# Both ends of a tree-attention kernel: codes fetched once, first V copies regrouped, one pair in other PSUM, three late stores on hardware queues

## The chip, the cores and the metric

The kernel runs on one core of one Trainium2 chip. The metric is the device time of one execution in microseconds; lower is better. Before the change the median of five runs is 138.11 us (137.77 to 138.54).

## What is computed

Attention over a binary tree: query i sees only itself and its ancestors. The shapes are 8 batches x 12 heads, 512 positions, 64 elements, all float32.

```python
mask = np.zeros((seq, seq))
for i in range(seq):
    mask[i, i] = 1
    parent = i
    while parent > 0:
        parent = (parent - 1) // 2
        mask[i, parent] = 1
scores = np.einsum('bhqd,bhkd->bhqk', Q, K) * scale
scores = scores + (1 - mask) * (-1e9)
weights = np.exp(scores - np.max(scores, axis=-1, keepdims=True))
weights = weights / (np.sum(weights, axis=-1, keepdims=True) + 1e-10)
return np.einsum('bhqk,bhkd->bhqd', weights, V)
```

## The kernel before

The 96 heads form 48 pairs (two heads, the unit of compute), 24 quads (four heads, the unit of a store) and 12 octets (eight heads, the unit of a V load and of the tile `vt`). Position n of a head sits on partition n // 4, slot n % 4, so one partition of one head is 1 KB in HBM.

For each pair i:
- `transpose(i)` (L280) makes 16 TensorE transposes of K and Q with the permutation tile `ptile` into the PSUM tile `kqp`; `evac(i)` (L293) copies it to SBUF on DVE.
- `scores1` and `scores2` (L309, L331): TensorE adds a product of mask codes (tiles `codes`, two copies on partitions 0 and 64 on, one for each head of a pair) and a product of keys and queries in PSUM, and ACT takes the exponential. No score matrix of 512x512 is made: a query sees at most ten keys, and the keys are sorted so that two groups of 128 are enough for each query tile.
- `values(i)` (L354): 20 products with 65 columns, the 65th a column of ones that gives the sum; they go to the PSUM tile `ob`, of which the pool has one.
- `norm(i)` (L380): DVE takes the reciprocal of the sums and multiplies into the output tile `of`.

V is not used as it was loaded. For each octet, copies bring rows of `vst` to where the products want them in `vt`: `spread_top` on POOL (L223), `spread_leaves` on DVE (L237), `spread_l7` on DVE or ACT (L250). Octet 0 is done in two halves by `spread_first` (L443); `spread_vector` (L451) says what DVE copies at which pair.

The order is written out by hand and no scheduler moves it. The main loop (L477) has at step i: scores of pair i, an ACT copy for some i, values and norm of pair i - 1, transposes of pair i + 2, DVE copies for some i, and further steps of POOL's program. The POOL program (L409) issues all K, Q and V loads but the first, which convert float32 to bfloat16 on the way, with 8 software DMAs at most under way, and all stores but the last; quad q is stored 8 quads behind its loads. After the last load come quads 14 to 17, the copies of octet 11, and quads 18 to 22. The last quad goes by SP (heads 0 and 1, then head 2) and ACT (head 3).

At the start SP and ACT load the first pair of K and Q, the permutations and both copies of the codes, while TensorE runs 12 products of zeros (`busy`, L474).

Of the kernel before, what the change touches and what calls it, by code (L numbers as in the profile page):

```python
# [41 lines left out]
KTOP, KLOW = 8, 40  # L42
# [61 lines left out]
def _permutations():  # L104

    eye = np.eye(128, dtype=np.float32)
    return np.concatenate([eye[:, r:r + 32] for r in PERMS], axis=1)


def _run(order):  # L110
    at = [n for n in range(len(PERMS) - 3) if PERMS[n:n + 4] == tuple(order)][0]
    return slice(32 * at, 32 * at + 128)
# [3 lines left out]
def kernel(  # L116
# [7 lines left out]
    nc = tc.nc  # L124
    B, H, S, D = Q.shape
    P = nc.NUM_PARTITIONS
    assert S == 512 and D == 64 and P == 128 and (B * H) % 4 == 0
    scale = float(1.0 / np.sqrt(D))
    NQ = B * H // 4
    NP = 2 * NQ  # L130

    fp32 = mybir.dt.float32
# [10 lines left out]
    perm_dram, top_dram, low_dram = (  # L143
        nc.inline_tensor(a.astype(ml_dtypes.bfloat16), name=name)
        for a, name in (
            (_permutations(), "permutations"), (top_np, "codes_top"), (low_np, "codes_low"),
        )
    )
# [11 lines left out]
    psT = ctx.enter_context(tc.tile_pool(name="psT", bufs=1, space=bass.MemoryType.PSUM))  # L160
    psO = ctx.enter_context(tc.tile_pool(name="psO", bufs=1, space=bass.MemoryType.PSUM))


    ptile = consts.tile([P, 32 * len(PERMS)], bf16)
    first = [consts.tile([P, 2, 4, D], fp32, name=f"first_{n}") for n in "kq"]
    codes = [
        consts.tile([P, a.shape[1]], bf16, name=f"codes_{n}")
        for n, a in enumerate((top_np, low_np))
    ]
    for tile_codes in codes:  # L170
        nc.vector.memset(tile_codes[:, :], 0.0)
    for eng, st, src in ((nc.sync, first[0], Kr), (nc.scalar, first[1], Qr)):
        eng.dma_start(out=st[:, :, :, :].rearrange("p h t d -> p h (t d)"), in_=src[:, 0:2, :])
    nc.sync.dma_start(out=ptile[:, :], in_=perm_dram.ap())
    for eng, half in ((nc.sync, 0), (nc.scalar, 64)):
        eng.dma_start(out=codes[0][half:half + KTOP, :], in_=top_dram.ap())
        eng.dma_start(out=codes[1][half:half + KLOW, :], in_=low_dram.ap())
    qperm = ptile[:, _run((0, 32, 64, 96))]
    perms = [ptile[:, _run(_slot_layout(t)[0])] for t in range(4)]
    k1code, q1code = codes[0][:, 0:128], codes[0][:, 128:640]  # L180
# [22 lines left out]
    qTs, kTs, kqps, obs, ets, ofs = {}, {}, {}, {}, {}, {}  # L203
# [10 lines left out]
    def load_k(o, h0=0, n=8):  # L214
        load(ksts, "kst", loads, Kr, o, h0, n)

    def load_q(o, h0=0, n=8):
        load(qsts, "qst", loads, Qr, o, h0, n)

    def load_v(o, h0=0, n=8):  # L220
        load(vsts, "vst", vloads, Vr, o, h0, n)
# [8 lines left out]
    def tile_pair(o, p, h0, h1, first):  # L230

        c, step = VCOL[first], VCOL[first + 2] - VCOL[first]
        return vts[o % NV][p:p + 64, h0:h1, c:c + 2 * step].rearrange(
            "p h (t d) -> p h t d", t=2
        )[:, :, :, 0:D]

    def spread_leaves(o, upper, h0=0, h1=8):  # L237

        nc.vector.tensor_copy(  # L239
            out=tile_pair(o, 64 if upper else 0, h0, h1, upper),  # L240
            in_=vsts[o][64:128, h0:h1, upper:3 + upper:2, :],
        )

    def swapped(src, step):

        return bass.AP(
            src.tensor, src.offset, [list(src.ap[0]), list(src.ap[1]), [step, 2], [1, D]]
        )

    def spread_l7(copy, o, quad, h0=0, h1=8):  # L250

        slot = 2 * (quad % 2)
        lower = quad < 2
        copy(  # L254
            out=tile_pair(o, 0, h0, h1, 1)[32 * quad:32 * quad + 32] if lower
            else tile_pair(o, 64, h0, h1, 0)[32 * quad - 64:32 * quad - 32],
            in_=swapped(vsts[o][32:64, h0:h1, slot + (not lower), :], D if lower else -D),
        )

    def busy(n):  # L260

        ob = psO.tile([P, 2, 512], fp32, name="ob")
        for _ in range(n):
            nc.tensor.matmul(  # L264
                out=ob[:, 0, :], lhsT=zeros[:, 0:128], rhs=zeros[:, :], start=True, stop=True
            )
# [86 lines left out]

    def values(i):  # L354

        obs[i] = ob = psO.tile([P, 2, 512], fp32, name="ob")
        e1, e2, vt = ets[i], e2s[i % NE], vts[(i // 4) % NV]

        def product(e, a, t, col, lo=0, hi=128, **flags):

            start_o = 65 * t + (t >= 2)
            col -= t < 2
            nc.tensor.matmul(  # L363
                out=ob[lo:hi, a, start_o:start_o + 65],
                lhsT=e[:, a, QPOS[t], lo:hi],
                rhs=vt[:, 2 * (i % 4) + a, col:col + 65],
                **flags,
            )

        for a in range(2):  # L370
            for t in range(4):
                product(e1, a, t, VTOP, start=t == 0, stop=False)
            for t in (2, 3):
                product(e2, a, t, VCOL[t], start=False, stop=False)
        for a in range(2):
            for t in (0, 1):
                product(e2, a, t, VCOL[SELF[t]], 0, 64, start=False, stop=t == 1)
                product(e2, a, t, VCOL[t], 64, 128, start=False, stop=t == 1)
# [20 lines left out]
    def store(eng, q, h0=0, n=4):  # L399
        eng.dma_start(  # L400
            out=Or[:, 4 * q + h0:4 * q + h0 + n, :],
            in_=ofs[q][:, h0:h0 + n, :, :].rearrange("p h t d -> p h (t d)"),
        )
# [3 lines left out]
    NO = NQ // 2  # L407

    def pool_program():  # L409

        load_k(0, 2, 2)
        load_q(0, 2, 2)
        load_v(0, 0, 4)
        load_k(0, 4, 4)
        load_q(0, 4, 4)
        load_v(0, 4, 4)
        load_k(1, 0, 4)
        load_q(1, 0, 4)
        spread_top(nc.gpsimd, 0, 0, 4)
        load_v(1)  # L420
        load_k(1, 4, 4)
        load_q(1, 4, 4)
        spread_top(nc.gpsimd, 0, 4, 8)
        yield
        yield
        for o in range(2, NO):
            load_k(o, 0, 4)
            load_q(o, 0, 4)
            load_v(o)
            load_k(o, 4, 4)  # L430
            spread_top(nc.gpsimd, o - 1)
            load_q(o, 4, 4)
            yield
            for q in (2 * o - BEHIND, 2 * o + 1 - BEHIND):
                if q >= 0:
                    store(nc.gpsimd, q)
        for q in range(NQ - BEHIND, NQ - 1):
            yield
            store(nc.gpsimd, q)
            if q == NQ - BEHIND + 1:  # L440
                spread_top(nc.gpsimd, NO - 1)

    def spread_first(quad, parts):  # L443

        for part in parts:
            if part < 4:
                spread_l7(nc.vector.tensor_copy, 0, part, 4 * quad, 4 * quad + 4)
            else:
                spread_leaves(0, part - 4, 4 * quad, 4 * quad + 4)

    def spread_vector(i):  # L451

        if i == 1 or i == 2:
            spread_first(1, range(3) if i == 1 else range(3, 6))
        o, step = divmod(i + 2, 4)
        if 1 <= o < NO:
            if step == 0:
                spread_leaves(o, 0)
            elif step == 1:
                spread_leaves(o, 1)  # L460
                for quad in (2, 3):
                    spread_l7(nc.vector.tensor_copy, o, quad)

    def pool_until(done, wanted):
        while done < wanted:
            next(program, None)
            done += 1
        return done
# [2 lines left out]
    steps = pool_until(0, 1)  # L471
    nc.vector.tensor_copy(out=ksts[0][:, 0:2, :, :], in_=first[0][:, :, :, :])
    nc.scalar.copy(out=qsts[0][:, 0:2, :, :], in_=first[1][:, :, :, :])
    busy(12)  # L474
    transpose(0)
    evac(0)
    for i in range(NP + 1):  # L477
        if i < NP:
            scores1(i)
            scores2(i)  # L480

            o, quad = divmod(i + 1, 4)
            if 1 <= o < NO and quad < 2:
                spread_l7(nc.scalar.copy, o, quad)
        if i == 1:
            transpose(2)
            evac(2)
            spread_first(0, range(4, 6))
        if i >= 1:
            values(i - 1)  # L490
            norm(i - 1)
        for n in (1 if i == 0 else i + 2,):
            if n < NP:
                transpose(n)
                evac(n)
        if i == 0:
            spread_first(0, range(4))
        spread_vector(i)
        if steps < NO:
            steps = pool_until(steps, min((i + 11) // 4, NO))  # L500
        else:
            steps = pool_until(steps, min(steps + 2, NO + (i - 2) // 2 - (NQ - 1 - BEHIND)))
        if i == NP - 1:
            store(nc.sync, NQ - 1, 0, 2)
    store(nc.sync, NQ - 1, 2, 1)
    store(nc.scalar, NQ - 1, 3, 1)

# [29 lines left out]
```

## Time and profile before

| what | value |
|---|---|
| median of five runs | 138.11 us |
| the profiled execution: its time, its span | 137.95 us, 135.9 us |
| busy: PE, DVE, ACT, POOL | 112.7, 103.7, 105.6, 95.3 us |
| read from HBM, written to it | 37.92 MB, 12.58 MB |
| DMA packets: software queue, two hardware queues | 30.68 MB; 0.77 and 0.44 MB |
| PE's waits for V copies on DVE | 3.3 us, 4 times |
| last Q load: issued; PE goes on with it | 110.99 us, 121.30 us |
| last multiply ends | 131.15 us |

The span runs from the first to the last instruction; about 2.05 us of the execution lie outside it. DMA shares can be over 1 because packets of one engine overlap. A row of the timeline has the start, the duration, the engine, the line, what it writes and reads, and in brackets what ended the idle time before it. A row of issues in the DMA view has the size and the time from issue to landing.

### The profile page before, as it was taken

How to read it: one execution, taken by the hardware profiler on the slowest of the kernel's cores; microseconds unless marked ns; L12 is line 12 of the kernel's file. 1: busy time of each engine (PE TensorE's matmuls, PEld its weight loads, DVE VectorE, ACT ScalarE, POOL GpSimd, SP SyncE). 2: the span in 40 equal slices, each digit the busy share in tenths (PEclk: the TensorE clock that was granted, in tenths of full speed). 3: DMA queues.
4: the chain of work that ended last, by engine and by line, in shares of the span. 5: the costliest groups of instructions: out<-in, count | busy, mean ns of one | idle time of the engine just before them, and what ended most of it. 6: DMA issues, size and time to landing. Idle time of an engine off the chain costs nothing.

```text
span 135.9 us, 5536 instructions
## 1 busy us (share of the span) xinstructions
PE 112.7 (83%) x2412; PEld 80.4 (59%) x2412; DVE 103.7 (76%) x220; ACT 105.6 (78%) x121; POOL 95.3 (70%) x140
## 2 busy tenths in 40 slices
PE   4985939999899898998998997997998697969620
PEld 1344716767576676775686674765766576747310
DVE  6139798879879879599698798898797878797520
ACT  3236554989989989989899899798899878898700
POOL 6969969397797975972985796596597597294200
PEclk9999995999999999999999999999999999999965
DMA  3999999999999999999999999999999999999981
GB/s 125 202 188 195 196 196 197 198 196 198 196 198 236 321 200 205 347 198 200 345 202 198 320 234 196 303 253 198 283 272 198 258 300 198 246 378 380 370 311 49
DMA packets 42043, 32.23 MB, mean 237 GB/s; under 512 B 1476, under 2 KB 39076, under 8 KB 42020
## 3 DMA queue, kind: packets, MB, share of 16 engines
q0 software_dynamic: 40640, 30.68, 124.6%
q1 hardware_dynamic: 898, 0.77, 1.7%
q10 hardware_dynamic: 482, 0.44, 1.0%
q8 instruction: 18, 0.29, 0.8%
q14 instruction: 5, 0.04, 0.1%
HBM read 37.92 MB, written 12.58 MB: 372 GB/s over the span
## 4 chain that ended last, share of the span: by engine, by line
PE 37%; ACT 22%; DMA 17%; DVE 14%; issue 4%; POOL 2%; ACTq 0%
PE ob L363 12%; DMA vst<-in_V_dram 9%; ACT e L324 9%; DMA qst<-in_Q_dram 8%; ACT e L348 7%; PE kqp L276 7%; ACT vt L254 5%; PE s L313 4%; PE ob L264 4%; PE s L335 4%; DVE of L392 4%; DVE vt L254 4%; PE s L342 3%; PE s L318 3%; DVE kq L302 3%
## 5 line engine op out<-in xcount | busy, mean ns | idle before, releaser
L324 ACT ACTIVATE e<-s 128x1024 bf16<-128x1024 f32 x48 | 49.0, 1021 | 17.1 <-PE s L318 16.3
L363 PE MATMUL ob<-vt,e 128*128 128x65 bf16 (+1 forms) x960 | 39.3, 198 | 10.2 <-DVE of L392 6.4
L363 PEld LDWEIGHTS <-e 128*128 128x128 bf16 (+1 forms) x960 | 31.1, 103 | 17.1 <-PE s L342 6.6
L348 ACT ACTIVATE e<-s 128x768 bf16<-128x768 f32 x48 | 38.4, 801 | 0.0
L225 POOL COPY vt<-vst 32x512 bf16<-32x512 bf16 (+1 forms) x52 | 31.0, 597 | 10.4 <-DMA vst<-in_V_dram 8.4
L302 DVE COPY kq<-kqp 128x1024 bf16<-128x1024 bf16 x48 | 32.7, 682 | 5.4 <-PE kqp L276 5.4
L392 DVE TENSOR_TENSOR of<-ob,rec 128x512 f32<-128x512 f32 x48 | 33.2, 692 | 1.7
L209 POOL DMA_DIRECT2D kst<-in_K_dram x24 | 18.3, 763 | 12.3 <-DMA vst<-in_V_dram 10.4
L254 ACT COPY vt<-vst 32x1024 bf16<-32x1024 bf16 x22 | 22.8, 1036 | 2.6 <-DVE vt L239 2.3
L389 DVE RECIPROCAL rec<-ob 128x8 f32<-128x8 f32 x48 | 9.9, 207 | 16.5 <-PE ob L363 15.6
L276 PE MATMUL kqp<-ptile,kst 128*64 128x128 bf16 x384 | 19.6, 222 | 1.5 <-issue 1.5
L209 POOL DMA_DIRECT2D qst<-in_Q_dram x24 | 18.2, 758 | 2.8 <-PE s L342 1.2
L400 POOL DMA_DIRECT2D out_dram<-of x23 | 17.4, 762 | 3.6 <-DVE of L392 3.2
L276 PE MATMUL kqp<-ptile,qst 128*64 128x128 bf16 x384 | 19.1, 221 | 1.0 <-DMA qst<-in_Q_dram 1.0
L318 PE MATMUL s<-kq 64*128 64x512 bf16 x96 | 19.0, 381 | 1.0 <-DVE kq L302 0.7
L313 PE MATMUL s<-codes 64*128 64x512 bf16 x96 | 19.0, 389 | 1.0 <-ACT e L324 0.2
L342 PEld LDWEIGHTS <-kq 64*128 64x128 bf16 x384 | 16.1, 95 | 5.0 <-issue 0.4
L342 PE MATMUL s<-kq 64*128 64x96 bf16 (+3 forms) x384 | 17.9, 211 | 0.0
L254 DVE COPY vt<-vst 32x1024 bf16<-32x1024 bf16 (+1 forms) x30 | 16.6, 553 | 0.7
L335 PE MATMUL s<-codes 64*128 64x384 bf16 x96 | 16.2, 328 | 1.0
L335 PEld LDWEIGHTS <-codes 64*128 64x128 bf16 x96 | 7.6, 94 | 12.6 <-issue 6.0
L276 PEld LDWEIGHTS <-qst 128*64 128x64 bf16 x384 | 13.7, 111 | 1.2 <-DMA qst<-in_Q_dram 1.2
(20 smaller groups left out, 59.1 us busy)
## 6 DMA issues: line engine op xcount, KB each, us to landing
out_dram<-of POOLq DMA_DIRECT2D x23, 512.0 KB, 10.5
kst<-in_K_dram POOLq DMA_DIRECT2D x23, 256.0 KB, 11.4
qst<-in_Q_dram POOLq DMA_DIRECT2D x23, 256.0 KB, 9.6
vst<-in_V_dram POOLq DMA_DIRECT2D x11, 512.0 KB, 12.6
vst<-in_V_dram POOLq DMA_DIRECT2D x2, 256.0 KB, 6.3
first_q<-in_Q_dram ACTq DMA_DIRECT2D x1, 256.0 KB, 3.6
first_k<-in_K_dram SPq DMA_DIRECT2D x1, 256.0 KB, 3.3
out_dram<-of SPq DMA_DIRECT2D x1, 256.0 KB, 4.8
```

The source lines that it names most:

```text
L209: nc.gpsimd.dma_start(out=kept[o][:, h0:h0 + n, :, :].rearrange("p h t d -> p h (t d)"), in_=src[:, 8 * o + h0:8 * o + h0 + n, :],)
L225: eng.tensor_copy(out=vts[o % NV][32 * j:32 * j + 32, h0:h1, VTOP:VTOP + D], in_=vsts[o][0:32, h0:h1, UNITS[TOP + j][1], :],)
L254: copy(out=tile_pair(o, 0, h0, h1, 1)[32 * quad:32 * quad + 32] if lower else tile_pair(o, 64, h0, h1, 0)[32 * quad - 64:32 * quad - 32], ...
L276: nc.tensor.transpose(out=dst, in_=st[i // 4][:, 2 * (i % 4) + a, t, :], identity=perm)
L302: nc.vector.tensor_copy(out=kq[:, :, :, :].rearrange("p k (x y) c -> p k x (y c)", x=2), in_=src)
L313: nc.tensor.matmul(out=sp[:, a, :], lhsT=k1code[64 * a:64 * a + 64, :], rhs=q1code[64 * a:64 * a + 64, :], start=True, stop=False,)
L324: nc.scalar.activation(out=et[:, :, :, :].rearrange("p a t c -> p (a t c)"), in_=sp[:, :, :].rearrange("p a c -> p (a c)"), func=AF.Exp, s ...
L335: nc.tensor.matmul(out=sp[:, a, :, 32:128], lhsT=k2code[64 * a:64 * a + 64, :], rhs=q2code[64 * a:64 * a + 64, :].rearrange("p (t c) -> p ...
L342: nc.tensor.matmul(out=sp[:, a, :, :].rearrange("p t c -> p (t c)")[:, lo:hi], lhsT=keys(i, a, TILE2[tile2]), rhs=qTs[i][64 * a:64 * a + 6 ...
L348: nc.scalar.activation(out=e2s[i % NE][:, :, :, 32:128].rearrange("p a t c -> p (a t) c"), in_=sp[:, :, :, 32:128].rearrange("p a t c -> p ...
L363: nc.tensor.matmul(out=ob[lo:hi, a, start_o:start_o + 65], lhsT=e[:, a, QPOS[t], lo:hi], rhs=vt[:, 2 * (i % 4) + a, col:col + 65], **flags,)
L392: nc.vector.tensor_tensor(out=ofs[q][:, 2 * r:2 * r + 2, :, :], in0=vals, in1=rec[:, :, :, :].to_broadcast([P, 2, 4, D]), op=ALU.mult,)
```

## The change

- Codes: fetched once, to partition 0 on, by SP; DVE copies them to partition 64 on. ACT issues the permutations ahead of its Q load.
- Start: nine products of zeros instead of twelve. All DVE copies of octet 0's first half stand behind the first transposes; its second half is shared by DVE and ACT; octet 1's copies stand at other steps. From octet 2 on the copies are as before.
- `values` of pair 46 writes into the `kqp` tile, which no transpose needs any more, instead of `ob`.
- Stores: quads 18 and 20 leave POOL for ACT's queue, two stores each, at steps 44 and 45; quad 22 for SP's queue, three stores, at step 46; of the last quad, heads 0 and 1 are two stores instead of one.

```diff
     for tile_codes in codes:
         nc.vector.memset(tile_codes[:, :], 0.0)
+    nc.scalar.dma_start(out=ptile[:, :], in_=perm_dram.ap())
     for eng, st, src in ((nc.sync, first[0], Kr), (nc.scalar, first[1], Qr)):
         eng.dma_start(out=st[:, :, :, :].rearrange("p h t d -> p h (t d)"), in_=src[:, 0:2, :])
-    nc.sync.dma_start(out=ptile[:, :], in_=perm_dram.ap())
-    for eng, half in ((nc.sync, 0), (nc.scalar, 64)):
-        eng.dma_start(out=codes[0][half:half + KTOP, :], in_=top_dram.ap())
-        eng.dma_start(out=codes[1][half:half + KLOW, :], in_=low_dram.ap())
+    for st, src, rows in zip(codes, (top_dram, low_dram), (KTOP, KLOW)):
+        nc.sync.dma_start(out=st[0:rows, :], in_=src.ap())
...
     def values(i):
-        obs[i] = ob = psO.tile([P, 2, 512], fp32, name="ob")
+        if i == NP - 2:
+            obs[i] = ob = psT.tile([P, 2, 512], fp32, name="kqp")
+        else:
+            obs[i] = ob = psO.tile([P, 2, 512], fp32, name="ob")
...
         for q in range(NQ - BEHIND, NQ - 1):
             yield
-            store(nc.gpsimd, q)
+            if q % 2 or q < NQ - 6:
+                store(nc.gpsimd, q)
...
     def spread_vector(i):
-        if i == 1 or i == 2:
-            spread_first(1, range(3) if i == 1 else range(3, 6))
-        o, step = divmod(i + 2, 4)
-        if 1 <= o < NO:
-            if step == 0:
-                spread_leaves(o, 0)
-            elif step == 1:
-                spread_leaves(o, 1)
-                for quad in (2, 3):
-                    spread_l7(nc.vector.tensor_copy, o, quad)
+        if i == 1:
+            spread_first(nc.vector.tensor_copy, 1, (4, 5))
+        o, step = divmod(i + (2 if i > 4 else 1), 4)
+        if 1 <= o < NO and step < 2:
+            if i <= 4:
+                parts = (0, 1) if step == 0 else (2, 3)
+            else:
+                parts = (0,) if step == 0 else (1, 2, 3)
+            for part in parts:
+                if part < 2:
+                    spread_leaves(o, part)
+                else:
+                    spread_l7(nc.vector.tensor_copy, o, part)
+
+    def spread_scalar(i):
+        if i == 1:
+            spread_first(nc.scalar.copy, 1, (0, 1))
+        o, quad = divmod(i + 1, 4)
+        if 2 <= o < NO and quad < 2:
+            spread_l7(nc.scalar.copy, o, quad)
+        if i == 4:
+            for quad in (0, 1):
+                spread_l7(nc.scalar.copy, 1, quad)
...
-    busy(12)
+    for st, rows in zip(codes, (KTOP, KLOW)):
+        nc.vector.tensor_copy(out=st[64:64 + rows, :], in_=st[0:rows, :])
+    busy(9)
...
             scores2(i)
-            o, quad = divmod(i + 1, 4)
-            if 1 <= o < NO and quad < 2:
-                spread_l7(nc.scalar.copy, o, quad)
+            spread_scalar(i)
         if i == 1:
             transpose(2)
             evac(2)
-            spread_first(0, range(4, 6))
+            spread_first(nc.vector.tensor_copy, 1, (2, 3))
...
         if i == 0:
-            spread_first(0, range(4))
+            spread_first(nc.vector.tensor_copy, 0, range(6))
         spread_vector(i)
...
+        if i in (NP - 4, NP - 3):
+            for h in (0, 2):
+                store(nc.scalar, NQ - 6 + 2 * (i - NP + 4), h, 2)
+        if i == NP - 2:
+            for h, n in ((0, 2), (2, 1), (3, 1)):
+                store(nc.sync, NQ - 2, h, n)
         if i == NP - 1:
-            store(nc.sync, NQ - 1, 0, 2)
+            for h in range(2):
+                store(nc.sync, NQ - 1, h, 1)
     store(nc.sync, NQ - 1, 2, 1)
     store(nc.scalar, NQ - 1, 3, 1)
```

(`spread_first` takes the copying engine's function as its first argument after the change.)

More of the change, by code (lines that the diff above doesn't have):

```diff
@@ L438, in pool_program, with spread_first @@
             yield
-            store(nc.gpsimd, q)
+            if q % 2 or q < NQ - 6:
+                store(nc.gpsimd, q)
             if q == NQ - BEHIND + 1:
                 spread_top(nc.gpsimd, NO - 1)
-    def spread_first(quad, parts):
+    def spread_first(copy, quad, parts):
         for part in parts:
             if part < 4:
-                spread_l7(nc.vector.tensor_copy, 0, part, 4 * quad, 4 * quad + 4)
+                spread_l7(copy, 0, part, 4 * quad, 4 * quad + 4)
             else:
```

## The prediction

> **What bounds it now.** I read the page's slices and queues first, then windows of the tail, then the timeline of the last 15 us with the DMA view, which gives each issue's time to landing.
>
> ```profile
> DMA  3999999999999999999999999999999999999981
> GB/s 125 202 188 195 196 196 197 198 196 198 196 198 236 321 200 205 347 198 200 345 202 198 320 234 196 303 253 198 283 272 198 258 300 198 246 378 380 370 311 49
> q0 software_dynamic: 40640, 30.68, 124.6%
> ```
>
> The DMA engines are full from the second slice to the last but one. At 198 GB/s written they load (float32 in, bf16 out); where stores mix in, the figure rises. Loads are 18.9 MB written, which at 0.197 MB/us is 96 us; stores are 12.6 MB at about 0.385, 33 us; together 129 of the 135.9 us. No compute engine is over 83% busy.
>
> Windows of the tail (PE, PEld, DVE, ACT, POOL busy, clock, DMA share, GB/s):
>
> ```profile
> 40.00:60.00 20.00, 18.82 (x440) 13.98 (x436) 16.47 (x36) 18.56 (x22) 15.88 (x23) 1.00 1.34 252
> 129.00:130.00 1.00, 0.71 (x20) 0.63 (x19) 0.00 (x0) 0.00 (x0) 0.00 (x0) 0.91 1.02 385
> 131.00:132.00 1.00, 0.00 (x0) 0.00 (x0) 0.15 (x1) 0.00 (x0) 0.00 (x0) 0.50 0.52 191
> 132.00:133.00 1.00, 0.00 (x0) 0.00 (x0) 0.00 (x0) 0.00 (x0) 0.00 (x0) 0.50 0.84 290
> 133.00:134.00 1.00, 0.00 (x0) 0.00 (x0) 0.00 (x0) 0.00 (x0) 0.00 (x0) 0.50 0.11 39
> ```
>
> The stream runs dry only after 131: some engines pause, a few still work at 133. Who arrives last there? Timeline of the tail, then landings from the DMA view:
>
> ```profile
> 121.30 0.41 PE L276 MATMUL kqp<-ptile,qst 128*64 128x128 bf16 x8 [1.03 <-DMA qst<-in_Q_dram]
> 126.93 0.79 PE L363 MATMUL ob<-vt,e 128*128 128x65 bf16 x20
> 126.94 0.76 POOL L400 DMA_DIRECT2D out_dram<-of  x1 [3.21 <-DVE of L392]
> 127.39 0.80 ACT L348 ACTIVATE e<-s 128x768 bf16<-128x768 f32 x1
> 128.72 2.82 SPq L400 DMA_DIRECT2D out_dram<-of  x2
> 128.84 0.19 PE L363 MATMUL ob<-vt,e 128*128 128x65 bf16 x1 [1.12 <-DVE of L392]
> 130.46 0.69 DVE L392 TENSOR_TENSOR of<-ob,rec 128x512 f32<-128x512 f32 x1
> 131.19 0.38 ACTq L400 DMA_DIRECT2D out_dram<-of  x1
> ```
> ```profile
> qst<-in_Q_dram POOLq DMA_DIRECT2D x1, 256.0 KB, 10.3
> out_dram<-of POOLq DMA_DIRECT2D x1, 512.0 KB, 6.0
> out_dram<-of SPq DMA_DIRECT2D x1, 256.0 KB, 4.8
> out_dram<-of ACTq DMA_DIRECT2D x1, 128.0 KB, 3.1
> ```
>
> The last Q load, issued at 110.99, lands at 121.3; the last software store, issued at 126.94, at 132.9. Nine stores lie between: (132.9 - 121.3)/9 = 1.29 us each, back to back (the single issues give 122.6, 123.9, 125.2, 126.4, 127.7 and so on). So the slowest DMA engine has no pause from the last load to 132.9 and then does quad 23's hardware stores until 133.9; the last lands at 131.19 + 3.07 = 134.26, and closing takes 1.6 us more. Compute gives its last result at 131.15. Both chains end nearly together, and the stream's has no slack.
>
> **The change, part by part.**
>
> *Start.* PE: three warm-up matmuls fewer, 5.28/12 = 0.44 us each, -1.3 us to the first transpose. DVE: two new copies of codes. The nearest rows are a 32x512 bf16 copy, 0.41, and the 128x512 cast, 0.55, so 0.8 to 1.1 us; they follow the K cast (ends 4.57) and end before the first evacuation is due (7.7 - 1.3 = 6.4): hidden. ACT issues the permutations (0.46) before first Q, whose cast moves from 4.33 to about 4.8, ahead of its transposes. The V copies regrouped aim at four PE waits on DVE copies (3.3 us by the waits view), after which the clock was 0.58 from 20 to 24 us. Two half-octet copies and octet 1's pair go to ACT at other steps, about the same work. Compute may lead by 3 to 5 us at pair 4. Worth to the end: 0. Loads and stores are issued by POOL in the same order up to the last load, and the DMA share (1.34 to 1.45) is full with or without that lead. In the tail PE anyway waits for the Q landing (1.03 us above). If loads were quicker, the lead would count.
>
> The one gain in the stream: codes are fetched once, not twice, 50 KB less; at the 208 to 335 GB/s of 3 to 5 us that is 0.15 to 0.24 us, or 0 if the slowest engine didn't carry them. I take -0.13.
>
> *Last but one pair.* values(46) writes PSUM freed by the last transposes, so values(47) no longer waits 1.12 us for norm(46). Late next is the second exp of pair 47, 127.39 + 0.80 = 128.19. The products that need it take about 0.6 us, to 128.85, then reciprocal and multiply as now (0.24 + 0.69): result at 129.85, not 131.15, and mostly at full clock. That is -1.3 us for compute; for the end 0, while the slowest engine still has stores to move until 133.9. It would be late only with a result after about 132.5.
>
> *Stores.* Quads 18 and 20 go out as two stores of two heads each on ACT's queue, 22 as three on SP's; POOL keeps 14 to 17, 19, 21. Issue cost: 0.41 (SP, 128.72) to 0.51 (ACT, first Q) each, four on ACT: 1.6 to 2.0 us. Queued behind them are the exps of pairs 45, 46, 47, and behind these PE. ACT has 0.61 us idle at 124.7, so between 0 (the sequencer issues while ACT computes) and +1.3 us on the last exp. Even +1.3 only returns the result to 131.15: hidden by the stores. SP had nothing queued. Each hardware store takes one of eight semaphores in turn, so SP's last store also waits for the landing of quad 22's first half, near 132.5; its own 2.9 us can overlap the engine's other work, 0 to +0.3.
>
> What counts is engine time per byte. Two windows of the DMA view, 124 to 128 (software stores) and 132.5 to 134 (hardware stores):
>
> ```profile
> q0 software_dynamic: 409, 1.50, 100.7%
> ...
> q10 hardware_dynamic: 105, 0.09, 17.7%
> q1 hardware_dynamic: 88, 0.07, 14.1%
> ```
>
> Software: 1.007 x 64 engine-us for 1.50 MB, 43 us per MB. Hardware: 31.8% of 24 engine-us for 0.16 MB, 47 to 48 us per MB, in packets of 1 KB where software has 4 KB. A quad is 0.0328 MB per engine: 1.41 against 1.55, +0.14; against the cadence of 1.29 it is +0.26. Three quads: +0.42 to +0.78. I take +0.42, since with all engines writing the software figure is 43.
>
> Two rules of the Trainium skill bear on this. "DMA: Bandwidth & Descriptors", Rules for kernel authors, says that spreading DMAs over issuing engines brings no bandwidth; by it the stores cost 0, by the rows +0.42. The same page, Queues, rings and completion order, says that each DMA engine takes turns between queues by packet. By that ACT's first store, which can leave at about 119.5 (the copy before it waits for nothing), would slow the last Q load by up to 0.4 us. The rows speak against it: SP's store of 128.72 landed at 133.5, after the software store issued 1.8 us before it, whose cadence stayed 1.3. I take the rows: 0 for the load.
>
> *Sum.* -0.13 + 0.42 = +0.3 us on a profiled time of 137.95 (span 135.9, 2.05 around it). The median of the five runs is 0.16 higher, 138.11, so 138.4.
>
> **Rivals.**
> Forecast, no change that counts: the stream binds, both compute gains are hidden. 138.4, own range 137.8 to 138.5. Chance 0.43.
>
> Faster: the slowest engine is not full, and the end follows the last result. For it: the DMA share of 0.52 at 131 to 132. Then the result at 129.85 is 1.3 us earlier, but the stores before it land by 132.9 at their cadence, and a quarter quad more takes 0.3 to 0.4: no landing before about 133.3, so 134.26 - 133.3 = 0.95 at most. 138.11 - 0.95 = 137.2. Against: the unbroken 1.29 cadence to 132.9. 0.24.
>
> Slower: hardware packets cost more when all 16 engines write. Price 3 x (hardware quad - 1.29): at 1.55 it is +0.78, no start gain, so 138.9. It decides from a quad of 1.43 us (+0.41). At the start two queues of such packets moved 266 GB/s at a share of 0.80, 48 us per MB, 1.57 us a quad, so it is near. Were ACT held in its issues until earlier stores drained, the last exps would add to this, to 139.4. 0.33.
>
> That the change doesn't do what it says: if ACT's stores left after the load in any case, nothing here moves.
>
> **Numbers.** A measurement of this kernel can tell about 0.3% (0.41 us). The range takes the lower half of the faster case and nearly all of the slower one: 137.2 to 139.2 leaves out about 0.2. Faster 0.24, same 0.43, slower 0.33.
>
> **What would show it.** Right: the last Q load still lands within 0.4 us of 121.3; PE's waits on V copies are gone before 20 us, but it waits longer for loads later; the last multiply ends near 130, and the last landing is at 134.3 to 134.8; hardware queues show 47 us per MB or more. Wrong: a last Q landing at 120.5 or earlier (the start fed the stream), or a last landing before 133.8 (the tail was bound by compute), or ACT's exps of pairs 46 and 47 spread by over 1.5 us with a last multiply after 132.5.

## The result and the profile after

The changed kernel takes 137.48 us (median of 43 runs, 136.94 to 138.65) against 138.21 (80 runs of before, 137.40 to 139.47): ratio 0.9952, 95% interval 0.9940 to 0.9964. It is faster by about 0.66 us, where the forecast was +0.3. Ratios here and below are taken over fast executions alone, those within 1.5% of the fastest of the same kernel.

The profiled execution took 137.89 us (span 135.8), 0.4 above its median, where the one of before took 137.95 (span 135.9), 0.3 below. Single profiles of these kernels scatter by about 0.5 us, so the two spans side by side show nothing; their parts do.

From the page of the changed kernel, the slices and the queues that answer to those of before:

```profile
GB/s 103 221 171 193 193 195 202 193 196 198 196 197 222 334 197 207 343 205 200 341 212 197 321 235 198 301 255 198 271 283 198 249 307 199 226 384 399 384 292 66
q0 software_dynamic: 40208, 29.10, 121.5%
q10 hardware_dynamic: 1648, 1.51, 3.2%
q1 hardware_dynamic: 1330, 1.23, 2.7%
q8 instruction: 18, 0.29, 0.8%
```

1.5 MB moved from the software queue to the hardware queues, the slices in the middle are nearly the same, and the tail peaks at 399 instead of 380. Then the tail in the timeline of the changed kernel:

```profile
127.51 5.25 SPq L403 DMA_DIRECT2D out_dram<-of  x5
...
128.18 0.80 ACT L347 ACTIVATE e<-s 128x768 bf16<-128x768 f32 x1
...
129.14 0.67 PE L366 MATMUL ob<-vt,e 128*128 128x65 bf16 x16 [0.40 <-ACT e L347]
...
130.09 0.69 DVE L395 TENSOR_TENSOR of<-ob,rec 128x512 f32<-128x512 f32 x1
130.82 0.35 ACTq L403 DMA_DIRECT2D out_dram<-of  x1
```

The 1.12 us in which PE waited for the multiply of pair 46 are gone; it now waits 0.40 for the second exponential of pair 47, as forecast. The last two stores, in the DMA view of the window from 131 us on:

```profile
out_dram<-of ACTq DMA_DIRECT2D x1, 128.0 KB, 3.7
out_dram<-of SPq DMA_DIRECT2D x1, 128.0 KB, 2.4
```

SP's last store left at 132.43, 1.65 us after the result, because its semaphore was still out with half of quad 22 (landed 132.37), and it landed last, at 134.86. In before the last landing was 134.25. So this execution's data came out *later*, and yet its span is not longer. The missing piece is the closing, the time from the last landing to the end of the span: 1.64 us in before, 0.91 here.

### The profile page after: what moved, and what is told of

Read it like the earlier page. It is cut to its first block, busy times and chain, and to the rows that moved or that the text cites. A ratio compares the mean times of both kernels' runs of the same rounds, so it can differ in the third digit from the quotient of the medians.

```text
span 135.8 us, 5540 instructions
## 1 busy us (share of the span) xinstructions
PE 113.3 (83%) x2409; PEld 80.9 (60%) x2409; DVE 102.8 (76%) x220; ACT 106.6 (79%) x123; POOL 93.0 (68%) x137
## 4 chain that ended last, share of the span: by engine, by line
PE 44%; DVE 23%; ACT 17%; issue 6%; DMA 4%; ACTq 0%
PE ob L366 16%; PE kqp L275 10%; ACT e L323 8%; DVE of L395 6%; ACT e L347 6%; PE s L312 6%; DVE vt L253 6%; DVE kq L301 5%; DVE vt L238 4%; DMA first_q<-in_Q_dram 4%; PE s L317 4%; PE s L341 4%; PE s L334 4%; ACT vt L253 3%; DVE rec L392 2%
## 5 line engine op out<-in xcount | busy, mean ns | idle before, releaser
L366 PE MATMUL ob<-vt,e 128*128 128x65 bf16 (+1 forms) x940 | 38.8, 198 | 8.2 <-DVE of L395 5.6
L395 DVE TENSOR_TENSOR of<-ob,rec 128x512 f32<-128x512 f32 x47 | 32.5, 691 | 1.6
L253 ACT COPY vt<-vst 32x1024 bf16<-32x1024 bf16 (+1 forms) x24 | 24.0, 1001 | 0.3
L275 PE MATMUL kqp<-ptile,qst 128*64 128x128 bf16 x384 | 19.9, 224 | 2.4 <-ACT qst L492 1.4
L275 PE MATMUL kqp<-ptile,kst 128*64 128x128 bf16 x384 | 20.2, 226 | 1.9 <-issue 1.8
L341 PE MATMUL s<-kq 64*128 64x128 bf16 (+3 forms) x384 | 18.0, 212 | 0.0
L403 POOL DMA_DIRECT2D out_dram<-of x20 | 15.4, 774 | 2.8 <-DVE of L395 1.9
L275 PEld LDWEIGHTS <-qst 128*64 128x64 bf16 x384 | 14.3, 114 | 3.0 <-ACT qst L492 1.6
L275 PEld LDWEIGHTS <-kst 128*64 128x64 bf16 x384 | 13.1, 114 | 3.3 <-issue 2.2
L253 DVE COPY vt<-vst 32x1024 bf16<-32x1024 bf16 (+1 forms) x28 | 13.9, 495 | 0.6
```

The source lines that it names most:

```text
L253: copy(out=tile_pair(o, 0, h0, h1, 1)[32 * quad:32 * quad + 32] if lower else tile_pair(o, 64, h0, h1, 0)[32 * quad - 64:32 * quad - 32], ...
L275: nc.tensor.transpose(out=dst, in_=st[i // 4][:, 2 * (i % 4) + a, t, :], identity=perm)
L341: nc.tensor.matmul(out=sp[:, a, :, :].rearrange("p t c -> p (t c)")[:, lo:hi], lhsT=keys(i, a, TILE2[tile2]), rhs=qTs[i][64 * a:64 * a + 6 ...
L366: nc.tensor.matmul(out=ob[lo:hi, a, start_o:start_o + 65], lhsT=e[:, a, QPOS[t], lo:hi], rhs=vt[:, 2 * (i % 4) + a, col:col + 65], **flags,)
L395: nc.vector.tensor_tensor(out=ofs[q][:, 2 * r:2 * r + 2, :, :], in0=vals, in1=rec[:, :, :, :].to_broadcast([P, 2, 4, D]), op=ALU.mult,)
```

## What lies behind the last landing

I saw this only when all runs were done, in the trace's rows of SP. A DMA tells of its landing by a semaphore, and the kernel has a fixed set of these, here called lanes. When a kernel ends, SP waits for the semaphores of all lanes, one after the other, in a fixed order; each check of a semaphore that has long been set takes 0.06 us. Hardware DMAs take their eight lanes in turn (numbers 107 to 118 in the rows), so how many of them a kernel has issued decides which lane the last store is on. Rows of the trace (start, engine, instruction):

```
before: last landing 134.253, on semaphore 107
134.269 SP waits 107    134.333 109    134.395 110    134.454 111
134.516 112    134.575 113    134.637 114    134.696 118    134.763 drain
135.310 POOL drain      135.701 POOL passes its last barrier

after: last landing 134.858, on semaphore 118
133.274 SP waits 109    133.336 110    133.511 111    133.849 112
134.191 116    134.543 117    134.875 118    134.942 drain
135.489 POOL drain      135.584 POOL passes its last barrier
```

In before the last store is on the first of the hardware lanes, and all the others, landed earlier, are checked after it: 0.51 us from landing to drain. In the changed kernel, with 16 hardware DMAs (10 before), it is on the last: 0.08. POOL's last steps take another 0.30 less, in every profile of a kernel with late stores on hardware queues (in c1 and d1, which have none, the 0.30 lies a step earlier); why, the trace doesn't show. Together -0.73 us. The waits view of SP has both parts (line, awaited, us in total, times, longest). Before:

```profile
SPq L532 <- DMA out_dram<-of: 2.6, 1, 2.6
SPq L532 <- PEq L532: 1.0, 2, 0.8
```

After:

```profile
SPq L559 <- DMA out_dram<-of: 1.5, 5, 0.3
SPq L559 <- PEq L559: 0.7, 2, 0.5
```

One wait of 2.6 us up to the last store, with the other lanes still to come, against five short ones that pass lanes as they land; and 1.0 against 0.7 us for the final barrier.

## The experiments

All ran in five rounds beside before. "us" is (ratio - 1) x 138.2 with its interval; "closing" is that of the kernel's one profile, and "rest" is us less the change of the closing.

| kernel | ratio, 95% interval | us | last landing | closing | rest |
|---|---|---|---|---|---|
| before | 1 | 0 | 134.25 | 1.64 | 0 |
| after | 0.9952, 0.9940 to 0.9964 | -0.66 ±0.17 | 134.86 | 0.91 | +0.07 |
| c1_start | 0.9983, 0.9960 to 1.0007 | -0.24 ±0.32 | 134.06 | 1.26 | +0.14 |
| c2_psum | 0.9985, 0.9958 to 1.0013 | -0.21 ±0.38 | 135.25 | 1.64 | -0.21 |
| c3_stores | 0.9989, 0.9960 to 1.0019 | -0.15 ±0.41 | 134.03 | 1.27 | +0.22 |
| c4_fewer | 0.9960, 0.9940 to 0.9980 | -0.55 ±0.28 | 135.33 | 1.04 | +0.05 |
| d1_start_psum | 0.9967, 0.9948 to 0.9987 | -0.46 ±0.27 | 135.01 | 1.26 | -0.08 |
| d2_psum_stores | 0.9996, 0.9968 to 1.0025 | -0.06 ±0.39 | 134.73 | 1.27 | +0.31 |
| d3_start_stores | 0.9984, 0.9954 to 1.0013 | -0.22 ±0.41 | 134.42 | 0.91 | +0.51 |
| g1_quad22_sw | 0.9978, 0.9956 to 1.0000 | -0.30 ±0.30 | 134.41 | 1.10 | +0.24 |
| h1_late2 | 0.9961, 0.9941 to 0.9981 | -0.54 ±0.28 | 135.79 | 0.92 | +0.18 |
| h2_late4 | 0.9989, 0.9965 to 1.0013 | -0.15 ±0.33 | 136.15 | 0.97 | +0.52 |
| x1_start_bytes | 1.0086, 1.0058 to 1.0115 | +1.19 ±0.39 | 135.75 | 1.27 | +1.56 |
| x2_mid_bytes | 1.0081, 1.0056 to 1.0107 | +1.12 ±0.35 | 136.29 | 1.27 | +1.49 |
| y1_no_codes_part | 1.0007, 0.9979 to 1.0035 | +0.10 ±0.39 | 135.42 | 1.27 | +0.47 |
| y2_no_v_part | 0.9955, 0.9935 to 0.9976 | -0.62 ±0.28 | 135.05 | 0.91 | +0.11 |
| y3_codes_nine | 1.0043, 1.0020 to 1.0066 | +0.59 ±0.32 | | 0.92 | +1.31 |
| y6_all_hw | 0.9963, 0.9945 to 0.9980 | -0.51 ±0.24 | 134.79 | 0.91 | +0.22 |
| z1_codes_only | 0.9956, 0.9934 to 0.9979 | -0.61 ±0.31 | 134.82 | 0.92 | +0.11 |
| z2_order_only | 0.9973, 0.9954 to 0.9993 | -0.37 ±0.27 | 134.41 | 1.27 | 0.00 |

The profiled execution of y3 took 140.23 us, 1.4 above its median, so its last landing is left out. For stores on the lanes that had carried the codes the trace pairs no landing with an issue; g1's last store is one of them, and its landing is the last update of its semaphore. My theories were, from the traces of before and after: A, the stream of bytes sets the end and mixed queues move it faster; B, the start feeds the stream; C, the end follows the last result. A theory of the closing was not among them, so the expectations don't speak of it.

**One part at a time.** c1 takes the diff's start alone (fetches, warm-ups, V copies), c2 its change in `values`, c3 its store lines. c4 is the changed kernel with

```diff
-            for h, n in ((0, 2), (2, 1), (3, 1)):
+            for h, n in ((0, 2), (2, 2)):
                 store(nc.sync, NQ - 2, h, n)
         if i == NP - 1:
-            for h in range(2):
-                store(nc.sync, NQ - 1, h, 1)
+            store(nc.sync, NQ - 1, 0, 2)
```

> Of the change only the start: codes fetched once and copied, permutations ahead of Q on ACT, nine warm-up products, the first V copies regrouped. My working (the stream sets the end): ratio 0.998 to 1.000, the last Q load lands within 0.3 us of 121.3. Rival (the start feeds the end): ratio about 0.995, the last Q load lands at 120.8 or earlier.

> Of the change only the values of pair 46 in the freed PSUM. My working (the slowest DMA engine has no pause, so an earlier last result is hidden): ratio 0.999 to 1.001, though the last multiply ends near 129.9. Rival (the end follows the last result): ratio 0.993 to 0.996, the last landing at 133.3 to 133.7.

> Of the change only the stores: quads 18 and 20 on ACT's queue, 22 on SP's. My working (hardware packets cost more engine time): ratio 1.002 to 1.005. Rival (two kinds of queue side by side move more than one): ratio 0.995 to 0.998, with 395 GB/s or more in the windows of 122 to 128 where the kernel before has 352 to 385.

> The changed kernel with two hardware stores fewer (quad 22 in two stores, heads 0 and 1 of quad 23 in one), so that SP's last store no longer takes a semaphore that is still busy. If that wait (to 132.4, for a result that is there at 130.8) sets the end: ratio to the kernel before 0.985 to 0.991. If the stream sets it anyway: 0.994 to 0.996, as the changed kernel.

None of the parts is clear of noise alone; the product of the three ratios, 0.9957, is close to the 0.9952 of all. c3 as a whole isn't the +0.42 of the forecast. c2's own profile does not show the earlier result that was expected of it: its last multiply ends at 131.41, because PE stood still after the first of pair 47's value products:

```profile
128.04 0.20 PE L366 MATMUL ob<-vt,e 128*128 128x65 bf16 x1
...
129.56 0.88 PE L366 MATMUL ob<-vt,e 128*128 128x65 bf16 x19 [1.31 <-issue]
```

The last section comes back to this wait. c4's last store no longer waits for quad 22 (it left at 130.38, right after the result), and nothing is gained: the lane wait seen above did not set the time.

**Two parts at a time, and one quad back.** d1, d2 and d3 join the parts in pairs. g1 gives quad 22 back to POOL:

```diff
-            if q % 2 or q < NQ - 6:
+            if q % 2 or q < NQ - 6 or q == NQ - 2:
                 store(nc.gpsimd, q)
...
-        if i == NP - 2:
-            for h, n in ((0, 2), (2, 1), (3, 1)):
-                store(nc.sync, NQ - 2, h, n)
```

> Start and PSUM edits, without the hardware stores. Theory A (the tail is a stream of bytes, and hardware queues beside the software queue move it faster: 396 to 413 GB/s against 352 to 385): with no mixing only the 50 KB of codes are gained, 0.1 to 0.2 us below the kernel before, ratio 0.999. Theory B (the start feeds the stream): 0.5 below, ratio 0.996. Theory C (the end follows the last result): also 0.5 to 0.6 below, 0.996.

> PSUM edit and hardware stores, with the start of before. Theory A: most of the gain of the whole change, 0.4 to 0.5 us below before, ratio 0.9965. Theory B: nothing, ratio 1.000. Theory C: 0.5 below, ratio 0.996.

> Start edits and hardware stores, pair 46's values still waiting as before, so the last result is 1.3 us later than in the changed kernel. Theory A: quad 23's stores come later, when the other stores are nearly gone; 0.2 to 0.4 below before, ratio 0.998. Theory B: 0.5 below, ratio 0.996. Theory C: no gain but the codes, ratio 0.999.

> The changed kernel with quad 22 back on the software queue as one store: hardware queues carry quads 18, 20 and 23. Theory A: the two kinds stay side by side longer and the stretch with hardware packets alone (129 to 133 us, 290 to 310 GB/s) gets shorter, so 0.1 to 0.3 us below the changed kernel, ratio to before 0.993 to 0.995. Theories B and C: as the changed kernel, 0.9952. The recorded sum (0.14 us more for each hardware quad) gives 0.14 below it.

Theory A, that the tail gains from two kinds of queue side by side, expected most of the gain in d2 and little in d1. It looks like the reverse: d1, without a single new hardware store, has -0.46, and d2 -0.06, though the 0.40 between them is not clear of its noise of 0.47. g1 missed too, at -0.30 where A wanted -0.7 to -1.0. Its end shows the order of lanes once more, with three lanes to check after the last landing and 0.26 us to the drain:

```
g1: last landing 134.409, on semaphore 112
134.096 SP waits 111    134.426 112    134.485 116    134.547 117
134.606 118    134.673 drain
```

The windows say what became of A. Before (PE, PEld, DVE, ACT, POOL busy, clock, DMA share, GB/s):

```profile
125.00:128.00 3.00, 2.53 (x54) 1.77 (x52) 1.28 (x4) 2.94 (x4) 0.76 (x1) 1.00 1.03 378
128.00:131.00 3.00, 1.05 (x20) 0.77 (x20) 1.44 (x3) 0.19 (x1) 0.00 (x0) 0.80 0.97 364
119.00:131.00 12.00, 8.34 (x184) 6.00 (x180) 8.17 (x17) 8.46 (x10) 5.40 (x8) 0.95 1.02 376
```

After:

```profile
125.00:128.00 3.00, 2.86 (x57) 1.99 (x54) 1.86 (x4) 2.67 (x4) 0.00 (x0) 1.00 1.06 393
128.00:131.00 3.00, 1.41 (x37) 1.02 (x33) 1.80 (x4) 0.98 (x2) 0.00 (x0) 1.00 0.92 328
...
119.00:131.00 12.00, 9.38 (x212) 6.75 (x205) 8.71 (x19) 9.60 (x12) 3.23 (x5) 1.00 1.02 376
```

Mixed queues do move more for a while (393 against 378), and it is given back as soon as fewer bytes are queued (328 against 364): 376 GB/s over the twelve microseconds in both, 377 in d1. There is no bandwidth in the mixing. The timeline of d1, where no hardware store disturbs, shows the PSUM edit at its full size, last result 129.94 against 131.15:

```profile
128.30 0.67 PE L365 MATMUL ob<-vt,e 128*128 128x65 bf16 x16 [0.30 <-ACT e L347]
...
129.25 0.69 DVE L394 TENSOR_TENSOR of<-ob,rec 128x512 f32<-128x512 f32 x1
```

**Is the last result hidden, and is the stream full?** h1 and h2 repeat the last multiply, which changes no value:

```diff
-        nc.vector.tensor_tensor(
+        for _ in range(3 if i == NP - 1 else 1):      # 5 in h2
+            nc.vector.tensor_tensor(
```

x1 loads four heads of V, 512 KB, into tiles that nobody reads, on SP's queue behind the codes; x2 has the same lines at step 16 of the main loop.

```diff
+    for n, st in enumerate(extra):
+        nc.sync.dma_start(
+            out=st[:, :, :, :].rearrange("p h t d -> p h (t d)"), in_=Vr[:, 2 * n:2 * n + 2, :]
+        )
```

> The changed kernel with the last multiply done three times over (the same result), so the last result comes 1.4 us later, about where the kernel before had it or 1 us behind. Theory A (the stream of stores sets the end, the last result is hidden up to about 132.5): 0 to 0.2 us above the changed kernel, ratio to before 0.995 to 0.997. Theory C (the end follows the last result one to one): 1.4 us above it, ratio 1.005.

> The same with the last multiply five times, so 2.8 us later, near 133.6. Theory A: the last store then runs alone, some 2.4 us from issue to landing (132.43 to 134.86 in the changed kernel), so a landing near 136.0, 1.1 to 1.5 us above the changed kernel, ratio 1.003 to 1.006. Theory C: 2.8 us above it, ratio 1.0155.

> The changed kernel with 512 KB more to load at the start, four heads of V that nobody reads, by SP's queue behind the codes. Theory A and B (the stream is full from the first microseconds, every byte at the start costs its time): at 0.25 to 0.39 MB/us 1.3 to 2.1 us above the changed kernel, ratio 1.005 to 1.010; 50 KB of codes are then worth a tenth of that. Rival: the start has room, or pauses later take it up: under 0.4 us, ratio under 0.998.

> The changed kernel with the same 512 KB loaded in the middle, when pair 16 is scored. Theory A (full stream): 1.3 to 2.6 us above the changed kernel, as much as at the start. Rival (the middle is paced by compute and has room): under 0.5 us.

In h1 the result comes at 132.61, later than in before:

```profile
130.47 2.14 DVE L396 TENSOR_TENSOR of<-ob,rec 128x512 f32<-128x512 f32 x3
132.65 0.35 ACTq L404 DMA_DIRECT2D out_dram<-of  x1
```

Its time is 0.12 us above the changed kernel's, within the noise. h2, 2.8 us later than unrepeated, costs 0.5. Theory C falls: the end does not follow the last result one to one, which has about 1.4 us to spare in the changed kernel. x2 missed its aim: nothing made SP wait, its loads left at 2.0 and 2.4 us, and so it repeats x1. Both cost 1.8 us over the changed kernel. Of that 0.36 is the closing (18 hardware DMAs, not 16), which leaves about 1.5 us for 0.52 MB, 2.8 us per MB: bytes at the start cost full price. Whether they do in the middle was not tried again.

**Which part of the start?** y1 has the fetches and warm-ups of before, y2 the V copies of before; all else is as changed. y3 adds eight fetches of the codes into spare tiles. y6 puts quads 19 and 21 on ACT's queue too:

```diff
+    for pair in spare:                                     # y3
+        for st, src, rows in zip(pair, (top_dram, low_dram), (KTOP, KLOW)):
+            nc.sync.dma_start(out=st[0:rows, :], in_=src.ap())
...
-            if q % 2 or q < NQ - 6:                        # y6
+            if q < NQ - 6:
                 store(nc.gpsimd, q)
...
-            for h in (0, 2):
-                store(nc.scalar, NQ - 6 + 2 * (i - NP + 4), h, 2)
+            for q in (0, 1):
+                store(nc.scalar, NQ - 6 + 2 * (i - NP + 4) + q)
```

> The changed kernel with the fetches of the start as before (permutations by SP, codes fetched twice, 12 warm-up matmuls), but V copies, PSUM and stores changed. Theory B in the form of bytes (512 KB at the start cost 1.85 us, so 50 KB 0.18 us, more if the codes' 8 and 40 rows lie on few of the engines): ratio to before 0.997 to 0.999. Theory V (the regrouped V copies bring the time): as the changed kernel, 0.995.

> The changed kernel with the V copies grouped as before; fetches, PSUM and stores changed. Bytes: as the changed kernel, ratio 0.995 to 0.9965. Theory V: 0.998 to 0.999.

> The changed kernel with the codes fetched eight times more into tiles nobody reads, 400 KB by SP's queue at the start. If a byte of codes costs what a byte of x1_start_bytes cost (1.85 us for 512 KB): 1.45 us above the changed kernel, ratio to before 1.0055. If the 8 and 40 rows lie on few DMA engines, the busiest of them carries 43 KB where the mean is 26: 2.0 to 2.4 us, ratio 1.010 to 1.0125, and 50 KB were worth 0.25 to 0.3 us in the change.

> The changed kernel with quads 19 and 21 on ACT's hardware queue too, each of quads 18 to 21 one store of 512 KB; the software queue ends with quad 17. The recorded step (0.14 us more for each hardware quad): 0.28 us above the changed kernel, ratio 0.997. If hardware packets alone move only the 290 to 310 GB/s seen after 129 us, six quads of 3.1 MB take 10 us from 126.5: over 1.5 us above, ratio 1.006 or more. If those figures only showed that little was queued: as the changed kernel, 0.995.

y2 equals the changed kernel: the regrouped V copies bring nothing. y1 has lost the whole gain: it is the fetches. But y3, whose closing is that of the changed kernel, prices eight sets of codes, 0.41 MB, at 1.25 us, 3.1 us per MB or 0.16 us a set, and does not bear out that they lie on few engines. That is the price of x1 once its closing is taken off. So the bytes of the codes are worth 0.16, not the 0.76 between y1 and the changed kernel. y6 leaves the software queue empty from 127 us on. Its DMA view from 127 to 129:

```profile
q10 hardware_dynamic: 536, 0.53, 75.4%
q1 hardware_dynamic: 235, 0.23, 32.6%
```

0.76 MB in 2 us, 380 GB/s in hardware packets alone, no less than the 377 of software packets. Engine time is 1.08 x 32 us / 0.76 MB = 45 us per MB, near my 47, but the share is above 1: packets of 1 KB overlap more, so engine time per byte is not time per byte.

**The two halves of the fetches.** z1 is y1 with the codes fetched once and copied by DVE; z2 is y1 with the permutations first, on ACT's queue, and 9 warm-ups.

> Of the start's fetches only the codes fetched once and copied by VectorE; permutations again by SP behind K, first Q first on ACT's queue, 12 warm-up matmuls; V copies, PSUM and stores as changed. Theory D (the 50 KB and the two DMAs saved are what the fetch part brings): ratio to before 0.995 to 0.9965, as the changed kernel. Theory E (it is the permutations landing first and the earlier start of PE): 0.998 to 1.000, as y1.

> The other half: permutations first on ACT's queue and 9 warm-up matmuls, but the codes fetched twice; V copies, PSUM and stores as changed. Theory D: 0.998 to 1.000. Theory E: 0.995 to 0.9965. Both about 0.9975: each brings a part.

z1 equals the changed kernel; z2 lies between. So the codes alone are enough for the whole gain; whether the order brings a part of it doesn't separate within ±0.3 us. What fits the size is the closing: fetching the codes once saves two hardware DMAs, z1 has 16 like the changed kernel, and y1 and z2 have 18, which puts the last store on the second lane (109) and leaves 0.45 us of checks instead of 0.08. 0.37 of closing and 0.16 of bytes make 0.53, where z1 is 0.71 ±0.5 below y1 and the changed kernel 0.29 ±0.3 below z2. One pair doesn't fit: y1 and z2 have the same closing, and are 0.47 ±0.47 apart.

How far this goes: no kernel changed the closing alone, and the end-to-end times don't prove it. A least-squares sum of parts over fifteen kernels (all of the table but before, h2, x1, x2 and y3; c4, h1 and y6 counted as the changed kernel, g1 as half of its stores) fits about as well without the closing (codes -0.30 ±0.16, PSUM -0.16 ±0.19, stores -0.10 ±0.18 us) as with it taken off first (codes +0.06 ±0.16, PSUM -0.15 ±0.19, stores +0.25 ±0.18). It can't tell the two apart: in these kernels the codes and the stores each shorten the closing by about 0.37. The closing itself is read from the trace's rows, and it repeats: kernels with the same hardware DMAs and the last landing on the same lane agree in it within 0.02 us.

The spans of the single executions say more than the times. The part of a time outside its span differs between kernels, on the mean from 1.80 us (d1) to 2.28 (c3), with 2.0 in before and after, and no run shows why. By mean span, c1 is 0.36 ±0.17 us below before, c2 0.04 ±0.22 above, c3 0.39 ±0.20 below and the changed kernel 0.67 ±0.13 below (against all executions of before that ran beside the experiments); the closing alone would give -0.38, 0, -0.37 and -0.73. The three kernels without late hardware stores follow it within 0.1 us. The twelve of the fit with such stores lie between 0.07 below it and 0.48 above, 0.19 above on the mean, so these stores may cost something, less than the +0.42 of the forecast; and y1 (+0.11 ±0.30, closing -0.37) and d2 (-0.04 ±0.20, closing -0.37) show nothing of the closing. That the closing is the main part is likely; it is not shown.

## Why the prediction was wrong

- **The step that failed**, as far as the traces show it, is "closing takes 1.6 us more", carried from before to after as a constant. It is 0.91 after the change. The forecast's sum was +0.29; with -0.73 for the closing it is -0.44, and measured is -0.66 ±0.17. The remaining difference, 0.2 us, is what the rest column has for the changed kernel, +0.07 ±0.17 against +0.29; the term that can take it is the +0.42 of the stores. How much of the 0.66 is the closing stays open (above).
- **Luck.** The measured 137.48 lies inside the range of 137.2 to 139.2. That is luck: the range reached so low for the rival in which the end follows the last result, and h1 speaks against it; in d1 a last result 1.2 us earlier than before's went with a last landing of 135.01, against 134.25.
- **Bound.** "The stream's has no slack": held (x1: 512 KB cost 1.5 us; h1: 1.4 us on the last result cost 0.1).
- **Start.** V copies 0: held (y2). Codes -0.13: 0.16 by y3. What I left out is that two DMAs fewer turn the lanes by two.
- **PSUM.** Last result at 129.85: 129.94 in d1, 130.78 in the changed kernel's profile, where ACT reached the last exponential later (128.18; the row of before has 127.39). Worth 0: -0.2 ±0.2 by the sums above, +0.04 ±0.22 by c2's span; h1 says it isn't the time of the last result.
- **Stores.** +0.42: between -0.10 ±0.18 and +0.25 ±0.18 by the two sums, so not settled; +0.78 is out. Its working was wrong in one point: the price came from a window in which the queues were nearly empty, and was taken as engine time where throughput decides. y6 beside d1 has five more hardware quads, +0.70 by my price, and is 0.05 ±0.37 faster, of which 0.35 is closing: +0.30 ±0.37 for the five.
- **Queues.** I read the rows as speaking against turns by packet, since the cadence of the software stores stayed at 1.3 us. In the changed kernel, with 256 KB stores of ACT beside them, software stores landed at 126.48, 128.95 and 131.42, 2.5 us apart (1.5 to 2.0 in most of the other kernels with such stores): they do share, as the rule that I set aside says (the Trainium skill, "DMA: Bandwidth & Descriptors", Queues, rings and completion order). That the turns go by packet no run here shows. The last Q load was spared for another reason than the one I gave: in c4 ACT's first store left at 119.31, about as forecast, but its first packet moved at 122.02, when the load had landed (121.30). The rule that spreading over issuing engines brings no bandwidth (the same page, Rules for kernel authors) held: 376, 376, 377 and 373 GB/s from 119 to 131 in before, after, d1 and y6.
- **ACT's issues.** 0, not +1.3: in the trace the issue of 121.03 (0.50 us) lies inside the exponential of 120.68 (1.01 us).

The signs I named for "wrong" (a last Q landing by 120.5, a last landing before 133.8, spread exponentials) did not appear: every one was a sign ahead of the last landing. Two of the signs for "right" were missed by a little: the last Q load landed at 120.80, 0.5 us early, and the last landing is 134.86.

## What to carry over

Follow the profile to the end of the span, not to the last landing: with stores on several queues, what is waited for at the end, and in which order, is work on the path, and counting DMAs shifts it. Before a gain of half a per cent is put down to an edit, take the parts of the tail (last result, last landing, closing) apart in every profile at hand. And make sure that the last landing is the last: in g1 the landings that the trace pairs with an issue end at 133.75, and the store that ends the kernel came at 134.41. What this change leaves open is a kernel in which two small DMAs more or fewer turn the lanes and nothing else; it would show the closing alone.

## What I had not expected of the hardware

- The closing is 0.91 to 1.64 us, by the lane of the last store, 0.06 us for each semaphore checked after it, and by POOL's 0.30.
- Packets of 16 KB on the instruction queue (q8 in the page), about every 6 us, take 0.9 to 1.0 us each. In the profile of c2 the gap between two software stores was 2.67 us instead of 1.29 at 130.05, with such a packet from 127.1 to 128.1; in d1 it was 2.21 at 133.57, with one from 130.5 to 131.5; in before one from 126.9 to 127.9 delayed none. My reading is that a store comes late where the packet falls on the DMA engine that is last; the views don't name the engine. The packets come at other places in each profile, and may explain a part of the scatter between single profiles.
- The same packets go with PE's waits. In the nineteen profiles used here the page's releaser "issue" stands on 71 waits of PE over 0.15 us, and every one of them ended 1.25 to 1.63 us after the end of such a packet: PE seems to wait for its next instructions. The longest is 1.36 us (h1, at 110.19). In c2 one of 1.31 us ended at 129.56 and took back most of the 1.3 us that the PSUM edit was to bring.
- Hardware packets of 1 KB alone moved as many bytes as software packets of 4 KB (380 and 377 GB/s), if enough of them were queued.
